# A second list for the unsplit weight loads, another bank for one tile, and a later transpose, in a two-layer hybrid decoder trunk

## The chip, the cores and the metric

The kernel runs on one core of a Trainium2 chip. The metric is the device time of one execution in microseconds (us). Before the change three runs took 644.15, 646.39 and 647.86 us, with a median of 646.39 us. A change of less than 0.5% (3.2 us) counts as no difference here.

The core has five engines that each work off their own list of instructions, in the order in which it was written: TensorE (PE, matrix products into PSUM), VectorE (DVE), ScalarE (ACT), GpSimd (POOL) and SyncE (SP), which issues nearly all transfers from HBM. They meet at semaphores.

## The reference, cut to what matters

Two layers, each of them a mixer and a feed-forward block, on x of 256 tokens by 1024 features:

```
proj = rmsnorm(x, norm_mix) @ w_in          # 1024 x 3476, its columns shared out to the head groups
qk   = silu(causal_conv([m_q, m_k], conv_qk))
y_m  = mlstm(qk, m_v, m_o, gates)           # chunked linear attention, 4 heads of 128
y_b  = moba(rope(rmsnorm(b_q)), ..)         # block attention; with 256 tokens, plain causal
y_n  = nsa(n_q, n_kc, n_vc, ..)             # three branches: compressed, selected, window
x    = x + [y_m, y_b, y_n] @ w_out
x    = x + square(relu(rmsnorm(x, norm_ffn) @ w_ff1)) @ w_ff2
```

The compressed branch of `nsa` runs blocks of 32 tokens, with `cmp_pe` added, through a small network (`cmp_w1` of 2048 x 128 for keys and for values, `cmp_w2`). These are the "compressed layer" of the change. The convolution vectors are `conv_qk`.

## The kernel before, in words

**Products in pieces.** Float32 products are made of faster ones. A weight piece arrives in a `raw` tile (4 buffers; 128 x 1024 floats at most). ACT casts it to `hi` (fp32r), DVE subtracts to get `lo`; each has 6 buffers. Each product is three matmuls, activation-high by hi, activation-high by lo, activation-low by hi (`passes`). A `raw` buffer is free again when its `lo` is made, a `hi` and `lo` pair when PE has used it. The pieces of `cmp_w1` are used as they come, without a split; they go into tiles `whole` (2 buffers), and the set of their numbers is also called `whole`.

**Groups.** A layer takes the columns of `w_in` in the order of `ORDER`: o1 (compressed inputs and NSA queries), o6 (output gates), o2 (NSA keys, values and gates), o3 (mLSTM gates and MoBA queries), c0 and c1 (compressed layer, first half), q0 (convolution inputs), c2 and c3 (second half), o4, q1, q2, q3, o5. `project` does a group named o: two tiles of 128 tokens (i = 0, 1), each of which sums over 8 slices of the features in one PSUM bank of the kind `acc` (2 of them); a tile's bank is free when its sums have been read out. `project_t` does a q group in one `acc` bank. All short-lived PSUM tiles are of the kind `wk` (6 banks). `compress` multiplies two `cmp_w1` pieces at a time.

**What sets the order.** The whole program is written by a planner, `Flow`. Every helper is a generator that yields operations, requests for buffers, and names of events to wait for. `Flow.run` keeps an estimated clock for each engine, and takes next the operation that could start first, or one of smaller rank that is ready nearly as soon. So an edit to one helper can change the order on all engines. The planner's clock sets the order only; on the chip each engine waits at its semaphores for as long as it takes.

**Loads.** One generator, `loads`, runs over all pieces in the order of their use, and requests a buffer, `raw` or `whole`, for each before it goes on to the next. The instructions of all loads stand on SP.

**Small vectors.** `first` loads `norm_mix`, then `norm_ffn` and `conv_qk` into a tile `dg` (2 buffers), has PE turn them (`wk<-ident,dg`) and copies them to `V`. `first_smalls` loads the gains of the head norms into `GB` by three broadcast DMAs (moba, nsa_q, nsa_k), scales two of them by 1/8 on DVE, and loads and turns `cmp_pe`.

Of the kernel before, what the change touches and what calls it, by code (L numbers as in the profile page):

```python
# [29 lines left out]
ORDER = ("o1", "o6", "o2", "o3", "c0", "c1", "q0", "c2", "c3", "o4", "q1", "q2", "q3", "o5")  # L30
# [114 lines left out]
class Flow:  # L145
# [16 lines left out]
    def add(self, gen, rank):  # L162
        self.procs.append([rank, gen, None, None, 0.0])
# [7 lines left out]
    def free(self, *tiles):  # L171
        for t in tiles:
            name = t.tensor.name
            self.places[self.owner.pop(name)].append(self.used.get(name, ("", 0.0))[1])
# [107 lines left out]
def body(ctx, tc, x, w_in, b_if, conv_qk, m_norm, moba_g, nsa_qg, nsa_kg, cmp_pe, cmp_w1, cmp_w2,  # L282
# [11 lines left out]
    done, free, add = flow.done, flow.free, flow.add  # L294
# [6 lines left out]
    def new(tag, *shape, dt=F32):  # L301
        return New(tag, (128, *shape), dt)

    def wk(*shape, count=1):
        return New("wk", (128, *(shape or (512,))), F32, count)
# [3 lines left out]
    def keep(tag, *shape, dt=F32, parts=128):  # L309

        if tag not in kept:
            kept[tag] = cp.tile([parts, *shape], dt, tag=tag, name=tag)
        return kept[tag]

    def tokens(i):
        return slice(i * 128, (i + 1) * 128)
# [107 lines left out]
    whole = {j for j, p in enumerate(pieces) if len(p[0]) == 2}  # L424
# [1 line left out]
    coming = [0, 0]  # L426
    taken = [0]

    def loads():
        for j, (srcs, kk, n) in enumerate(pieces):  # L430
            if j < 4:
                yield f"x0{j % 2}{j // 2}"
            raw = yield new("whole" if j in whole else "raw", 1024)
            raws[j] = raw
            for src, a in srcs:
                dst = raw[:, :kk * n] if a is None else raw[:, a * 512:(a + 1) * 512]
                yield sy.dma_start(dst.rearrange("p (k n) -> p k n", n=n), src)
            done.add(f"raw {j}")
# [36 lines left out]
    def weights():  # L475

        j = taken[0]
        taken[0] += 1
        yield f"lo {j}"
        if j >= SPLIT0:  # L480
            yield f"los {j}"
        _, kk, n = pieces[j]
        t = parts.pop(j)
        return tuple(a[:, :kk * n].rearrange("p (k n) -> p k n", k=kk) for a in t) + (t,)
# [48 lines left out]
    def passes(po, hx, lx, wh, wl, first, last):  # L533
        yield mm(po, hx, wh, start=first, stop=False)
        yield mm(po, hx, wl, start=False, stop=False)
        yield mm(po, lx, wh, start=False, stop=last)

    def project(l, name, n):

        L = Ls[l]  # L540
        po = L.o.setdefault(name, [])
        ws = []
        order = [(i, k) for i in range(2) for k in range(8)]
        if l == 0 and name == ORDER[0]:

            order = [(i, 2 * j + k) for j in range(4) for i in range(2) for k in range(2)]
        for i, k in order:
            if k == 0:
                po.append((yield new("acc", 512)))
            yield f"H{l}{i}{k}"  # L550
            if len(ws) == k // 2:
                ws.append((yield from weights()))
            elif l == 0 and name == ORDER[0] and k // 2 < SPLIT0:
                yield f"los {k // 2}"
            wh, wl, t = ws[k // 2]
            hx, lx = (a[:, k, tokens(i)] for a in (L.Hh, L.Hl))
            yield from passes(po[i][:, :n], hx, lx, wh[:, k % 2, :], wl[:, k % 2, :], k == 0, k == 7)
            done.add("started")
            if i and k % 2:
                free(*t)  # L560
            if k == 7:
                done.add(f"{name}{l}{i}")
# [148 lines left out]
    def main():  # L711
        for l in range(DEPTH):
            for name in ORDER:
                if name in ("c0", "c2"):
                    yield from compress(l, int(name[1]))
                elif name[0] == "c":
                    continue
                elif name[0] == "q":
                    yield from project_t(l, int(name[1]))
                else:  # L720
                    yield from project(l, name, GROUPS[name][1])
            yield from out_project(l)
            yield from feed_forward(l)
# [4 lines left out]
    def first():  # L728
        yield sy.dma_start(ident, cst[:, 0:128])
        v = (yield new("dg", 128))  # L730
        yield ac.dma_start(v[0:16], norm_mix.rearrange("l (k p) -> (l k) p", p=128))

        warm = keep("warm", 1)
        yield gp.memset(warm, 0.0)
        yield act(warm, warm, AF.Exp)
        for h in range(2):
            c = slice(h * 512, (h + 1) * 512)
            for i in range(2):
                yield sy.dma_start(xs[i][:, c], x[tokens(i), c])
                done.add(f"x0{i}{h}")  # L740
                yield f"raw {2 * h + i}"
        yield dv.memset(ones, 1.0)
        yield dv.memset(negh, -0.5)
        yield gp.memset(Ls[0].mr.bitcast(F32), 0.0)

        vps = yield wk()
        yield tr(vps[:, :16], v[:16], ident[:16, :16])
        yield dv.tensor_copy(V[:, :16], vps[:, :16])
        free(vps)
        done.add("V")  # L750
        yield "started"
        yield sy.dma_start(v[16:32], norm_ffn.rearrange("l (k p) -> (l k) p", p=128))
        yield sy.dma_start(v[32:96], conv_qk.rearrange("l j (c p) -> (l j c) p", p=128))
        vps = yield wk()
        yield tr(vps[:, :NV], v[:NV], ident[:NV, :NV])
        yield dv.tensor_copy(V[:, 16:], vps[:, 16:NV])
        free(vps, v)
        done.add("V2")
# [551 lines left out]

    tiles = [(i, n) for i in range(2) for n in range(2)]
    add(first(), -1)
    add(warm_up(), 101)
    for i, n in tiles:
# [4 lines left out]
    for l in range(DEPTH):  # L1319
# [4 lines left out]
        gens += [mlstm(l)] + [conv(l, c) for c in range(4)] + [attention(l, moba), score(l, moba)]  # L1324
        for g in gens:
            add(g, 2 + len(flow.procs))
    add(loads(), 95)

    def turn(j, ahead):

# [31 lines left out]
```

## Time and profile before

| | |
|---|---|
| three runs | 644.15, 646.39, 647.86 us |
| the profiled execution | 643.21 us |
| its span, first to last instruction | 641.4 us |
| PE busy (matmul) | 632.2 us, 99% |
| DVE, ACT busy | 442.8 us (69%), 368.9 us (58%) |
| granted TensorE clock, mean | 0.999 |

The profiled execution lies 1.81 us above its span and 3.18 us below the median of the three runs. In the timeline a row is a run of equal instructions: start in us from the span's start, time from the start of the first to the end of the last, engine, line, operation, output<-inputs, size, count, and in brackets the idle time of the engine just before and what ended it. Nearly all instructions have line L137, where the planner's wrapper calls the engine, so that tiles tell them apart. Matmuls are pipelined: a row's time is longer than the step from one start to the next.

### The profile page before, as it was taken

To read this page: it belongs to the slowest core of one execution; us is meant where nothing else is said; L and a number is where in the kernel's file an instruction comes from. 1 tells how busy PE (TensorE), PEld (TensorE's weight loads), DVE (VectorE), ACT (ScalarE), POOL (GpSimd) and SP (SyncE) were. 2 spreads that over 40 slices of the span, in tenths; PEclk is the share of its full clock that TensorE was granted. 3 is DMA by queue.
4 is the path that set the end of the run, shared out by engine and by line. 5 is a ranking of instruction groups with operands and counts; after the bars stand their busy time and mean duration, and the time that the engine had idled before them with its cause. 6 is when DMAs were issued, how large, how long until landed. Compare 5 with 4: busy or idle time off the path is not lost.

```text
span 641.4 us, 10239 instructions
## 1 busy us (share of the span) xinstructions
PE 632.2 (99%) x3815; PEld 544.5 (85%) x3815; DVE 442.8 (69%) x823; ACT 368.9 (58%) x718; POOL 30.9 (5%) x50
## 2 busy tenths in 40 slices
PE   9999999999999999999999999999999999999997
PEld 8788898888888888888899978988888888888885
DVE  6667898678666565656584689987776565665661
ACT  6659796547464454545384797856555553545440
POOL 1020300100000000000010111001000000000000
PEclk9999999999999999999999999999999999999999
DMA  8876724446646465655446654354566656574621
GB/s 270 221 217 205 207 92 159 137 132 228 218 154 223 158 226 169 200 195 184 144 131 183 216 167 129 103 175 127 159 230 191 203 171 215 161 225 150 223 71 66
DMA packets 79090, 112.78 MB, mean 176 GB/s; under 512 B 4896, under 2 KB 61248, under 8 KB 79040
## 3 DMA queue, kind: packets, MB, share of 16 engines
q1 hardware_dynamic: 79008, 112.12, 55.6%
q8 instruction: 30, 0.49, 0.3%
q14 instruction: 20, 0.16, 0.1%
q10 hardware_dynamic: 32, 0.01, 0.0%
HBM read 111.06 MB, written 1.05 MB: 175 GB/s over the span
## 4 chain that ended last, share of the span: by engine, by line
PE 85%; ACT 4%; DMA 3%; DVE 3%; issue 2%; POOL 1%; SPq 1%; DVEq 0%; POOLq 0%; ACTq 0%
PE wk L137 53%; PE acc L137 32%; DMA raw<-in_w_in 2%; DVE lo L137 1%; ACT hi L137 1%; ACT P L137 1%; DMA x<-in_x 1%; POOL hr L137 1%; SPq L136 1%; DMA dg<-in_cmp_pe 1%; DVE N L137 1%; ACT L137 1%; ACT QK L137 0%; ACT W L137 0%; DVE P L137 0%
## 5 line engine op out<-in xcount | busy, mean ns | idle before, releaser
L137 DVE TENSOR_TENSOR lo<-raw,hi 128x1024 fp32r<-128x1024 f32 (+4 forms) x209 | 240.5, 1167 | 124.7 <-ACT hi L137 123.9
L137 ACT CAST hi<-raw 128x1024 fp32r<-128x1024 f32 (+3 forms) x207 | 205.8, 1016 | 138.2 <-PE wk L137 110.8
L137 PE MATMUL wk<-H,hi 128*128 128x512 f32 x512 | 128.0, 391 | 0.0
L137 PEld LDWEIGHTS wk<-H,hi 128*128 128x128 f32 x512 | 93.7, 188 | 17.9
L137 PE MATMUL acc<-hi,H 128*128 128x512 f32 (+3 forms) x384 | 104.9, 353 | 0.5 <-ACT R L137 0.5
L137 PE MATMUL acc<-hi,P 128*128 128x512 f32 x240 | 79.3, 391 | 0.1
L137 PE MATMUL wk<-hi,P 128*128 128x512 f32 x240 | 78.8, 389 | 0.0
L137 PEld LDWEIGHTS wk<-H,lo 128*128 128x128 f32 x512 | 69.9, 190 | 5.0
L137 PEld LDWEIGHTS acc<-hi,H 128*128 128x128 f32 x384 | 66.9, 188 | 7.4 <-ACT R L137 0.8
L137 PE MATMUL wk<-H,lo 128*128 128x256 f32 x512 | 71.4, 282 | 0.0
L137 PE MATMUL acc<-lo,H 128*128 128x512 f32 (+3 forms) x192 | 68.3, 356 | 0.5 <-DVE lo L137 0.4
L137 PEld LDWEIGHTS acc<-hi,P 128*128 128x128 f32 x240 | 45.0, 188 | 9.4 <-DVE P L137 0.7
L137 PEld LDWEIGHTS wk<-hi,P 128*128 128x128 f32 x240 | 45.1, 188 | 9.3
L137 PE MATMUL acc<-H,hi 128*128 128x256 f32 x256 | 50.1, 288 | 1.1 <-ACT R L137 1.1
L137 PE MATMUL acc<-lo,P 128*128 128x512 f32 x120 | 47.0, 392 | 0.0
L137 PE MATMUL wk<-lo,P 128*128 128x512 f32 x120 | 46.7, 389 | 0.0
L137 ACT COPY th<-wk 128x256 f32<-128x256 f32 x64 | 23.8, 372 | 33.8 <-PE wk L137 33.8
L137 PEld LDWEIGHTS acc<-H,hi 128*128 128x128 f32 x256 | 40.1, 190 | 1.6 <-ACT R L137 1.3
L137 PEld LDWEIGHTS acc<-lo,H 128*128 128x128 f32 x192 | 36.1, 188 | 4.6 <-DVE lo L137 1.0
L137 PE MATMUL acc<-H,lo 128*128 128x256 f32 x128 | 37.5, 293 | 0.0
L137 ACT ACTIVATE H<-wk,V 128x128 fp32r<-128x128 f32 x64 | 18.5, 372 | 24.2 <-PE wk L137 24.2
L137 ACT CAST P<-cv 128x512 fp32r<-128x512 f32 x30 | 18.7, 622 | 17.5 <-DVE cv L137 17.5
(194 smaller groups left out, 790.2 us busy)
## 6 DMA issues: line engine op xcount, KB each, us to landing
raw<-in_w_ff SPq DMA_DIRECT2D x128, 512.0 KB, 4.3
raw<-in_w_in SPq DMA_DIRECT2D x40, 512.0 KB, 4.3
raw<-in_w_out SPq DMA_DIRECT2D x16, 512.0 KB, 3.5
whole<-in_cmp_w SPq DMA_DIRECT2D x16, 256.0 KB, 4.5
raw<-in_w_in SPq DMA_DIRECT2D x8, 384.0 KB, 4.2
raw<-in_w_in SPq DMA_DIRECT2D x8, 268.0 KB, 3.3
raw<-in_w_in SPq DMA_DIRECT2D x8, 264.0 KB, 3.6
x<-in_x SPq DMA_DIRECT2D x4, 256.0 KB, 5.3
```

The costliest lines, as they stand in the source:

```text
L136: return Op(self.name, lambda: f(out, *args), outs, [], 0.0)
L137: o = Op(self.name, lambda: f(out, *args, **kw), outs, ins, self.cost(op, outs, ins))
```

## The change

It has three parts.

1. `loads` takes a flag and is added twice. The first copy loads the split pieces, the second, with a smaller rank, the unsplit ones (`whole`). The second waits before each unsplit piece until the piece ahead of it in the common order has been issued. So a split piece no longer stands behind an unsplit one that lacks a buffer.
2. In layer 0 the tile i = 0 of the second group (o6) takes a `wk` bank instead of an `acc` bank.
3. The turn of `norm_ffn` and `conv_qk` in `first` waits until the event o600, the end of that same tile.

```
-    def loads():
+    def loads(unsplit):
         for j, (srcs, kk, n) in enumerate(pieces):
+            if (j in whole) != unsplit:
+                continue
             if j < 4:
                 yield f"x0{j % 2}{j // 2}"
+            elif unsplit:
+                yield f"raw {j - 1}"
             raw = yield new("whole" if j in whole else "raw", 1024)
...
             if k == 0:
-                po.append((yield new("acc", 512)))
+                po.append((yield new("wk" if l == 0 and name == ORDER[1] and i == 0 else "acc", 512)))
...
         yield sy.dma_start(v[32:96], conv_qk.rearrange("l j (c p) -> (l j c) p", p=128))
+        yield f"{ORDER[1]}00"
         vps = yield wk()
         yield tr(vps[:, :NV], v[:NV], ident[:NV, :NV])
...
-    add(loads(), 95)
+    add(loads(False), 95)
+    add(loads(True), 94)
```

The instructions are the same in number (3559 matmuls of the program's own count, before and now). The order changes at many places; four pieces of it matter below. Numbers behind a name tell buffers apart; they differ between the two programs.

**DVE, group o6 of layer 0.** The names `lo_334` to `lo_389` before, and `lo_331` to `lo_396` now, are the four pieces of o6. Before:

```order
L137 TENSOR_SCALAR dg_339<-ident_79,rs1_94 128x128
L137 TENSOR_TENSOR lo_334<-raw_219,hi_299 128x1024
L137 TENSOR_TENSOR lo_352<-raw_249,hi_333 128x1024
L137 TENSOR_TENSOR lo_380<-raw_289,hi_349 128x1024
L137 TENSOR_SCALAR GB_91<-GB_91 128x2x64
L137 TENSOR_TENSOR lo_389<-raw_316,hi_379 128x1024
```

Now:

```order
L137 TENSOR_SCALAR dg_336<-ident_79,rs1_94 128x128
L137 TENSOR_TENSOR lo_331<-raw_219,hi_297 128x1024
L137 TENSOR_TENSOR lo_350<-raw_248,hi_330 128x1024
L137 TENSOR_SCALAR GB_91<-GB_91 128x2x64
L137 TENSOR_TENSOR lo_381<-raw_288,hi_346 128x1024
L137 TENSOR_TENSOR lo_396<-raw_313,hi_380 128x1024
```

The scaling of `GB` stood behind the split of the third piece and now stands ahead of it.

**PE, the end of o6's first tile.** The tile is `acc_370` before and `wk_360` now; `dg_399` and `dg_392` hold `cmp_pe`, `dg_106` the convolution vectors. Before:

```order
L137 MATMUL acc_370<-lo_380,H_70 128x512
L137 MATMUL acc_370<-hi_349,H_70 128x512
L137 MATMUL acc_370<-hi_379,H_70 128x512
L137 MATMUL acc_370<-lo_389,H_70 128x512
L137 MATMUL wk_401<-ident_79,dg_399 128x64
L137 MATMUL acc_370<-hi_379,H_70 128x512 x2
L137 MATMUL acc_370<-lo_389,H_70 128x512
L137 MATMUL acc_370<-hi_379,H_70 128x512
```

Now:

```order
L137 MATMUL wk_360<-lo_381,H_70 128x512
L137 MATMUL wk_360<-hi_346,H_70 128x512
L137 MATMUL wk_360<-hi_380,H_70 128x512
L137 MATMUL wk_394<-ident_79,dg_392 128x64
L137 MATMUL wk_360<-lo_396,H_70 128x512
L137 MATMUL wk_360<-hi_380,H_70 128x512
L137 MATMUL wk_422<-ident_79,KV_344 128x128
L137 MATMUL wk_422<-ident_79,KV_369 128x128
L137 MATMUL wk_360<-hi_380,H_70 128x512
L137 MATMUL wk_360<-lo_396,H_70 128x512
L137 MATMUL wk_360<-hi_380,H_70 128x512
L137 MATMUL wk_435<-ident_79,dg_106 128x96
```

The turn of `cmp_pe` stood behind 20 matmuls of the tile and now stands behind 19; the turn of the convolution vectors, which stood in group o1, follows the tile.

**SP, from q0 to o4 of layer 0.** The 128x4x256 loads are q0's pieces, the 128x2x512 loads o4's, `whole` those of c2 and c3. Before:

```order
L136 DMA raw_514<-in_w_in 128x4x256
L136 DMA raw_521<-in_w_in 128x4x256
L136 DMA whole_687<-in_cmp_w1 128x4x128 x2
L136 DMA whole_704<-in_cmp_w1 128x4x128 x2
L136 DMA raw_718<-in_w_in 128x2x512
L136 DMA raw_729<-in_w_in 128x2x512
L136 DMA raw_747<-in_w_in 128x2x512
```

Now:

```order
L136 DMA raw_493<-in_w_in 128x4x256
L136 DMA raw_523<-in_w_in 128x4x256
L136 DMA raw_563<-in_w_in 128x2x512
L136 DMA raw_580<-in_w_in 128x2x512
L136 DMA raw_635<-in_w_in 128x2x512
L136 DMA whole_695<-in_cmp_w1 128x4x128 x2
L136 DMA whole_715<-in_cmp_w1 128x4x128 x2
```

Three of o4's loads have moved ahead of those of c2 and c3. In layer 1 the same rows have moved in the same way.

**ACT, from q0's casts to the read-out of o3's first tile, layer 0.** `hi_570`, `hi_605` before and `hi_571`, `hi_611` now are q0's pieces; `hi_642`, `hi_657` are o4's first two; `R_694<-acc_580` and `R_706<-acc_583` read out o3's first tile. Before:

```order
L137 CAST hi_570<-raw_514 128x1024
L137 CAST hi_605<-raw_521 128x1024
L137 COPY N_552<-N_552 128x4x48
L137 COPY KV_653<-N_552 128x256
L137 COPY N_594<-N_594 128x4x48
L137 ACTIVATE R_694<-acc_580,rs0_93 128x256
L137 COPY KV_697<-N_594 128x256
L137 COPY QK_73<-wk_689 128x4x128
L137 COPY QK_73<-wk_713 128x2x128
```

Now:

```order
L137 COPY N_552<-N_552 128x4x48
L137 CAST hi_611<-raw_523 128x1024
L137 CAST hi_642<-raw_563 128x1024
L137 COPY KV_662<-N_552 128x256
L137 COPY N_598<-N_598 128x4x48
L137 CAST hi_657<-raw_580 128x1024
L137 COPY KV_708<-N_598 128x256
L137 COPY QK_73<-wk_701 128x4x128
L137 COPY QK_73<-wk_721 128x2x128
L137 ACTIVATE GT0_101<-GT0_101 128x12
L137 ACTIVATE R_706<-acc_583,rs0_93 128x256
```

The read-out stood ahead of the copy `KV` and of the two copies to `QK`; it now stands behind them and behind the casts of two pieces of o4.

## Rows read from the trace of the kernel before

**Rows 1.** The page, part 1: busy us (share of the span) xinstructions.

```profile
PE 632.2 (99%) x3815; PEld 544.5 (85%) x3815; DVE 442.8 (69%) x823; ACT 368.9 (58%) x718; POOL 30.9 (5%) x50
```

**Rows 2.** Waits of PE: who waited for whom, us in total, times, longest us.

```profile
PE acc L137 <- ACT R L137: 1.5, 2, 1.1
...
PE wk L137 <- DVE PcT L137: 0.5, 1, 0.5
PE acc L137 <- DVE lo L137: 0.4, 1, 0.4
PE wk L137 <- DMA dg<-in_cmp_pe: 0.3, 1, 0.3
```

**Rows 3.** Timeline of PE, group o6, first tile, layer 0.

```profile
18.54 0.50 PE L137 MATMUL acc<-hi,H 128*128 128x512 f32 x1 [0.46 <-ACT R L137]
...
21.68 0.40 PE L137 MATMUL acc<-lo,H 128*128 128x512 f32 x1
...
23.05 0.39 PE L137 MATMUL acc<-lo,H 128*128 128x512 f32 x1
23.70 0.27 PE L137 MATMUL wk<-ident,dg 64*128 64x64 f32 x1 [0.26 <-DMA dg<-in_cmp_pe]
23.90 0.73 PE L137 MATMUL acc<-hi,H 128*128 128x512 f32 x2
```

**Rows 4.** Timeline of SP, the loads of nsa_q's gains and of cmp_pe.

```profile
16.50 0.43 SPq L136 DMA_DIRECT2D GB<-in_nsa_q_norm  x1
...
19.43 0.50 SPq L136 DMA_DIRECT2D dg<-in_cmp_pe  x1
```

**Rows 5.** DMA issues of 16 to 19.9 us: KB each, median us from issue to landing.

```profile
GB<-in_nsa_q_norm SPq DMA_DIRECT2D x1, 32.0 KB, 4.7
dg<-in_cmp_pe SPq DMA_DIRECT2D x1, 32.0 KB, 4.2
```

**Rows 6.** Timeline of DVE, third piece of o6 and the scaling of GB.

```profile
20.19 1.23 DVE L137 TENSOR_TENSOR lo<-raw,hi 128x1024 fp32r<-128x1024 f32 x1 [1.26 <-ACT hi L137]
21.34 0.22 DVE L137 TENSOR_SCALAR GB<-GB 128x128 f32<-128x128 f32 x1
```

**Rows 7.** Timeline of PE, the turn of the convolution vectors in o1.

```profile
12.14 0.59 PE L137 MATMUL acc<-hi,H 128*128 128x384 f32 x2
12.58 0.25 PE L137 MATMUL wk<-ident,dg 96*128 96x96 f32 x1
12.60 0.42 PE L137 MATMUL acc<-lo,H 128*128 128x384 f32 x1
12.86 0.51 PE L137 MATMUL acc<-hi,H 128*128 128x384 f32 x2
```

**Rows 8.** Timeline of ACT, from q0's casts to the copies to QK, layer 0.

```profile
40.63 1.05 ACT L137 CAST hi<-raw 128x1024 fp32r<-128x1024 f32 x1 [2.70 <-DMA raw<-in_w_in]
41.97 1.05 ACT L137 CAST hi<-raw 128x1024 fp32r<-128x1024 f32 x1 [0.28 <-DMA raw<-in_w_in]
...
43.82 0.40 ACT L137 COPY KV<-N 128x256 f32<-128x256 f32 x1 [0.56 <-DVE N L137]
...
45.27 0.47 ACT L137 ACTIVATE R<-acc,rs 128x256 f32<-128x256 f32 x1 [0.73 <-DVE GI L137]
...
45.94 1.11 ACT L137 COPY QK<-wk 128x512 f32<-128x512 f32 x2
```

**Rows 9.** Timeline of PE, start of q0, second half of the compressed layer, o4.

```profile
45.80 0.50 PE L137 MATMUL acc<-H,hi 128*128 128x256 f32 x2 [1.08 <-ACT R L137]
...
55.11 1.08 PE L137 MATMUL wk<-whole,MQ 128*32 128x128 f32 x32
...
57.90 0.50 PE L137 MATMUL acc<-lo,H 128*128 128x512 f32 x1 [0.42 <-DVE lo L137]
```

**Rows 10.** Timeline of SP, the loads of q0, then of c2 and c3.

```profile
34.18 2.32 SPq L136 DMA_DIRECT2D raw<-in_w_in  x2
43.33 2.02 SPq L136 DMA_DIRECT2D whole<-in_cmp_w  x4
```

## The prediction

> **What bounds the kernel now.** Read the busy times first: PE is busy for 632.2 of 641.4 us [rows 1]. A change that leaves the matmuls as they are can win only what PE waits, so the second view is PE's waits. The longest entries are small: 1.5 us on ACT's read-out R in two waits, 0.5 on a copy PcT, 0.4 on a lo, 0.3 on the load of cmp_pe [rows 2]. The third view is PE's timeline, which says where they lie. The two waits on R are the first matmul of o6, idle 0.46 us [rows 3], and the first of q0, idle 1.08 us [rows 9]; together they are all of the 1.5, so layer 1 has no such wait. The lo wait is o4's second matmul [rows 9], the load wait the turn of cmp_pe inside o6 [rows 3]. Last come ACT, DVE and SP around these places, since they decide what is late next.
>
> What the change aims at is thus 0.46 (the bank), 0.26 (the turn of cmp_pe) and 0.42 (o4's pieces): 1.1 us, 0.2% of the time. What it can lose is not bounded that way, because it rearranges in-order engines that feed PE.
>
> **Part 1, group o6: bank and convolution vectors.** The turn of the convolution vectors leaves o1: between 12.14 and 12.86 PE does three matmuls and that turn in 0.72 us [rows 7]. A 512-column matmul takes 0.228 (six from 21.68 to 23.05 [rows 3]), so three of 384 columns are an estimated 0.51 and the turn costs 0.2. Without it and without the idle 0.46, o6 starts 0.66 us sooner, at 17.88. The fourteenth matmul, the first that reads the third piece's lo, came 3.14 us after the start, at 21.68 [rows 3], and could now come at 21.02. But that lo ends at 20.19 + 1.23 = 21.42 [rows 6], and its cast on ACT is not moved. Even with DVE's order as it was, only 0.26 of the 0.66 is left.
>
> DVE's order is not as it was: the scaling of GB now stands ahead of that lo. It waits for the gains of nsa_q, issued at 16.50 [rows 4] and landed 4.7 us later [rows 5], at 21.2. The rows before hide this, as the scaling came at 21.34, behind the lo [rows 6]. Now DVE, which was idle for 1.26 us before that lo [rows 6], stands at the scaling until 21.2, and behind it are queued the third and fourth lo, for which PE waits. The scaling takes 0.22, overlapping the next by 0.08 as before [rows 6], so the lo runs from 21.35 to 22.6, and the fourteenth matmul comes at 22.6, not 21.68. Six steps on, at 22.6 + 6 x 0.228 = 23.97, stands the turn of cmp_pe, whose load (19.43 [rows 4] + 4.2 [rows 5] = 23.6) is in by then: its idle 0.26 is gone, in the shadow of the larger wait. Before, that turn came at 23.70 with 20 matmuls done [rows 3]; now 0.27 later with 19, which is 0.50 behind. The turn of the convolution vectors comes back for 0.2. Part 1 as a whole: 0.7 us late. Bounds: if nsa_q lands as fast as cmp_pe, 4.2, then 0.4; if it takes as much longer, 1.2. I take 0.7, by its own row.
>
> Here a rule speaks the other way. The Trainium skill, page "DMA: Bandwidth & Descriptors", section "Anatomy of one DMA — SWDGE (gpsimd) path", gives a DMA as about 2.0 us fixed plus bytes over 436 GB/s, fitted on the GpSimd path. By it nsa_q's 32 KB would land at an estimated 18.6 and cmp_pe's at 21.5, and block nothing: the fourteenth matmul would follow the lo's end at 21.45, the turn six steps later at 22.8 without a wait, and part 1 would win an estimated 0.45. Those loads took 4.7 and 4.2 us here [rows 5], among other loads of SP's queue, and I go by these.
>
> The later V copy on DVE is needed by the convolution after q0 and hidden there; if that cover went, it would cost its few tenths. The wk bank lent to o6 leaves five for short-lived tiles during 6 us in which few are open; I cost it at nothing, and a missing bank would show as a wait of the size of those seen, 0.3 to 0.5 [rows 2].
>
> **Part 2, q0: loads of o4 ahead.** Before, SP was done with q0's loads at 34.18 + 2.32 = 36.5 and stood until 43.33, for a `whole` buffer [rows 10]. Now o4's first two loads fill that gap. q0's casts both start on a landing, 40.63 and 41.97, so a 512 KB piece lands every 1.34 us [rows 8]; o4's first two would land at 43.3 and 44.65. Part 1 shifts PE by 0.7, and with it the casts that need PE's buffers and the loads behind them: 44.0 and 45.35. The shift could be 0 (if the queue, not the buffers, sets the loads) or 1.2.
>
> The planner now writes the casts of these pieces ahead of work that PE needs. ACT takes the first at 44.0 to 45.05, then KV (0.40) and a copy of that kind, then the second, until then landed, from 45.8. Behind it stand KV 0.40, two QK copies 1.11, a short GT of 0.2, and only then the read-out R of 0.47 [rows 8], whose bank q0's first matmul waits for. Neighbours on ACT overlap by 0.1 (R and KV, 0.47 and 0.40, fill 45.27 to 45.94, 0.67). So R ends at 45.8 + 1.05 + 0.40 + 1.11 + 0.2 + 0.47 - 0.5 = 48.55. PE followed R's end by 0.06 (45.74 to 45.80), so q0 starts at 48.6 instead of 45.80 [rows 9]: 2.8 us late, part 1's 0.7 included. Bounds: with the loads not shifted 2.1; with both casts waiting on nothing, their 2 us alone, 1.9; with the full 1.2 shift 3.3. The old wait of 1.08 stays inside: it grows, it does not go.
>
> c2 and c3 are now loaded behind three o4 loads. Their issue ended at 43.33 + 2.02 = 45.35 and PE used them at 55.11: 9.8 us of cover [rows 9, 10]. Three loads at 1.34 take 4.0 of it, and PE is later itself, so this costs nothing. Were the cover gone, each us beyond it would be one of PE.
>
> **Part 3, o4.** Its pieces are split long before use, so the idle 0.42 [rows 9] goes, with 0.1 for the restart: 0.5 won.
>
> **Layer 1.** Only the loads part acts there. By the order, one cast of o4, not two, stands ahead of R; PE did not wait for R there. I take 0. Bounds: 0.5 won (the PcT wait [rows 2]) and 2 lost.
>
> **Sum.** 2.8 - 0.5 = 2.3 us late. 643.2 + 2.3 = 645.5 for an execution like the profiled one; that one lies 3.2 below the median of its three runs, so 648.7, +0.35%.
>
> **The rivals.**
>
> A: the change does what it aims at. PE's three waits of 1.1 us go and nothing takes their place: 646.4 - 1.1 = 645.3. For it: the rows of the waits. Against it: the 0.26 cap of part 1, and the casts on ACT.
>
> B: part 1 as forecast, but ACT gets to R as early as before, because o4's pieces land well before their casts and DVE, which it waited for (0.73 on GI [rows 8]), had room for them; that idle time speaks for it. Then 0.7 - 0.5 = 0.2 late: 646.6. Against it: the landings 1.34 apart leave no room.
>
> C, slower: layer 1 pays as well. Place: q0 of layer 1, where the same three o4 loads have moved ahead. Price: the two casts ahead of PE's work, 1.05 each [rows 8], 2.1 us more: 650.8, +0.7%. It decides from the point where R, or DVE's work for the gates behind the o4 splits, ends after PE has come to q0. Against it: no wait on R there before, and loads that run further ahead.
>
> D: the two small loads are in early, nsa_q before 20.19, when DVE took the third lo [rows 6], and cmp_pe before its turn. Part 1 then wins instead of losing, but q0 starts where o4's landings put it, 2.1 late (part 2's bound without a shift): 2.1 - 0.5 = 1.6 late, 648.0. For it: such a small load has little to move. Against it: 4.7 and 4.2 us in the rows [rows 5]. The Trainium skill's rule for one DMA, above, is on this side.
>
> **How the numbers follow.** Forecast 0.55, A 0.12, B 0.14, C 0.14, D 0.05. The forecast's own range is 646.6 to 650.4: its bounds, and about 1 us for a median of runs that differ by 3.7. The range for 8 in 10 is 645.0 to 651.0. Faster by over 0.5% means under 643.2, which asks for more than all the aimed waits: 0.04. Slower by over 0.5% means above 649.6: a quarter of the forecast, most of C and a little of B and D, 0.27. Within 0.5%: 0.69.
>
> **What would show it.** In o6, DVE idle of about 2 us ahead of the scaling of GB, released by a DMA, and PE waiting for a lo of about 1.5 us; against it, a scaling that starts before 19.5. At q0, PE idle of 3 us before its first matmul, released by ACT's R, with two casts of o4 ended by landings before it; against it, q0 starting within 1.5 us of 45.8. At o4, no wait on a lo. The forecast is wrong if PE's waits in sum are smaller than before, or if layer 1 has a wait of over 1 us of its own.

## The result, and the profile after

The changed kernel took 650.73 us (median of 14 executions, 647.83 to 653.32), the kernel before, on the same chip, 643.98 us (14 executions). The ratio is 1.0094, with a 95% interval of 1.0078 to 1.0111: about 6.1 us slower by the ratio (the two medians lie 6.75 apart), and more than the 0.5% that counts. The forecast, 2.3 us slower and 648.7 us, had the sign, but called it most likely too small to tell.

The profiled execution took 649.26 us, with a span of 647.5 us against 641.4. Two parts of the page of the changed kernel: busy time of PE, which answers to [rows 1], and the granted clock in 40 slices of the span.

```profile
PE 634.5 (98%) x3815; PEld 546.8 (84%) x3815; DVE 443.5 (68%) x823; ACT 368.5 (57%) x718; POOL 31.2 (5%) x50
...
PEclk9997999999999999999999999999999999999999
```

PE is busy 2.3 us longer with the same matmuls. The 7 in the fourth slice says that they ran there at a lower clock; before, all 40 digits are 9. Next, PE's waits of the changed kernel (in total, times, longest), against [rows 2]:

```profile
PE acc L137 <- ACT R L137: 2.1, 1, 2.1
PE wk L137 <- DVE lo L137: 2.0, 1, 2.0
PE wk L137 <- ACT KV L137: 1.8, 1, 1.8
```

The load of cmp_pe and the lo of o4 are gone, as meant. In their place stand a lo of 2.0 in a `wk` tile (that is o6), a KV of 1.8, and one R of 2.1. Where they lie is read from the starts of PE's rows in layer 0:

| PE starts, us | before | after | later by |
|---|---|---|---|
| o6 | 18.54 | 17.66 | -0.89 |
| o2 | 30.88 | 31.85 | +0.97 |
| compressed layer, first half | 42.62 | 43.59 | +0.97 |
| q0 | 45.80 | 49.57 | +3.77 |
| compressed layer, second half | 55.11 | 61.44 | +6.33 |
| o4 | 56.54 | 62.45 | +5.91 |
| feed-forward | 146.17 | 152.32 | +6.15 |
| layer 1, q0 | 359.09 | 365.57 | +6.48 |
| last matmul | 636.49 | 642.64 | +6.15 |

There are three steps: 0.97 in o6, 2.80 in front of q0, and 2.56 between q0 and the second half of the compressed layer, where nothing waits that did not wait before. After that, all is moved as a block, within 0.4 us. (o4's 5.91 is a change of order: four transposes, 0.42 us, stood between the second half and o4's first matmul, and now stand behind it.)

**The step in o6.** DVE's timeline of the changed kernel (start, time, engine, line, operation, tiles, count, idle time before) answers to [rows 6]:

```profile
21.38 0.23 DVE L137 TENSOR_SCALAR GB<-GB 128x128 f32<-128x128 f32 x1 [2.59 <-DMA GB<-in_nsa_q_norm]
21.52 2.98 DVE L137 TENSOR_TENSOR lo<-raw,hi 128x1024 fp32r<-128x1024 f32 x3
```

SP's timeline of the same kernel, against [rows 4], with the next load of a piece:

```profile
16.36 0.43 SPq L136 DMA_DIRECT2D GB<-in_nsa_q_norm  x1
...
22.77 1.50 SPq L136 DMA_DIRECT2D raw<-in_w_in  x2
```

PE's timeline, against [rows 3], with the turn of cmp_pe in the second row:

```profile
22.79 0.50 PE L137 MATMUL wk<-lo,H 128*128 128x512 f32 x1 [2.01 <-DVE lo L137]
...
24.38 0.27 PE L137 MATMUL wk<-ident,dg 64*128 64x64 f32 x1
```

DVE stands 2.59 us at the scaling of GB until nsa_q's gains land, 4.93 us after their issue at 16.36 (at 21.29), with the third and fourth lo behind it. PE waits 2.01 us for the third. There is a second effect that the forecast left out: a `raw` buffer comes free when its lo is made, and SP's next load of a piece goes out at 22.77 instead of 21.45 (over the whole span, 393.6 us of SP's waits are for a lo). The view by windows shows what the transfers lose. Its columns are the stretch and its length, busy time and count of PE, PEld, DVE, ACT and POOL, granted clock, DMA share and GB/s. Of the kernel before:

```profile
22.00:24.00 2.00, 1.74 (x9) 1.09 (x7) 1.20 (x2) 1.08 (x2) 0.00 (x0) 1.00 0.80 214
```

And of the changed kernel:

```profile
22.00:24.00 2.00, 1.21 (x5) 1.03 (x6) 2.00 (x3) 1.04 (x2) 0.00 (x0) 1.00 0.33 63
```

214 GB/s fell to 63 in that window. Loads follow each other closely up to q0, whose first one goes out at 36.59 instead of 34.18. It landed at 42.66, not 40.61: 2.05 us late, where PE was only 0.97 late.

**The step at q0.** ACT's timeline of the changed kernel, against [rows 8]:

```profile
42.69 1.05 ACT L137 CAST hi<-raw 128x1024 fp32r<-128x1024 f32 x1 [2.95 <-DMA raw<-in_w_in]
...
44.05 1.05 ACT L137 CAST hi<-raw 128x1024 fp32r<-128x1024 f32 x1
45.43 1.04 ACT L137 CAST hi<-raw 128x1024 fp32r<-128x1024 f32 x1 [0.33 <-DMA raw<-in_w_in]
46.38 0.40 ACT L137 COPY KV<-N 128x256 f32<-128x256 f32 x1
...
46.94 1.04 ACT L137 CAST hi<-raw 128x1024 fp32r<-128x1024 f32 x1
47.88 0.40 ACT L137 COPY KV<-N 128x256 f32<-128x256 f32 x1
48.19 0.84 ACT L137 COPY QK<-wk 128x512 f32<-128x512 f32 x2
48.93 0.22 ACT L137 ACTIVATE GT<-GT 128x12 f32<-128x12 f32 x1
49.05 0.47 ACT L137 ACTIVATE R<-acc,rs 128x256 f32<-128x256 f32 x1
```

And PE's, against [rows 9]:

```profile
46.83 0.44 PE L137 MATMUL wk<-ident,KV 128*128 128x128 f32 x2 [1.79 <-ACT KV L137]
47.10 0.39 PE L137 MATMUL wk<-ident,N 128*128 128x128 f32 x2
49.57 0.80 PE L137 MATMUL acc<-H,hi 128*128 128x256 f32 x2 [2.07 <-ACT R L137]
```

The first two casts are q0's, the next two (45.43, 46.94) o4's. KV stands behind the first of these, R behind both, and behind another KV, two QK copies and GT. PE waits 1.79 us for KV and 2.07 for R, with 0.66 us of transposes between.

**The step behind q0.** The windows of the changed kernel show the cause in the third column from the end, the granted clock:

```profile
46.00:48.00 2.00, 0.66 (x4) 0.40 (x4) 2.00 (x12) 2.00 (x5) 0.00 (x0) 1.00 0.95 247
48.00:50.00 2.00, 0.43 (x2) 0.43 (x3) 2.00 (x6) 2.00 (x6) 0.00 (x0) 0.71 1.13 341
50.00:52.00 2.00, 2.00 (x11) 1.67 (x12) 2.00 (x7) 1.03 (x3) 0.00 (x0) 0.50 1.11 370
...
54.00:56.00 2.00, 2.00 (x16) 2.00 (x15) 1.24 (x3) 0.79 (x3) 0.00 (x0) 0.58 1.04 355
56.00:58.00 2.00, 2.00 (x20) 2.00 (x19) 0.30 (x3) 1.99 (x7) 0.00 (x0) 1.00 0.42 149
```

Towards the end of the two waits, before q0's first matmul, the clock falls from 1.00 to 0.50, that is from 2.4 to 1.2 GHz, and is back only from 56 us on. A 256-column matmul then takes a step of 0.21 us instead of 0.12. From q0's first matmul to the second half of the compressed layer the same work, but for two transposes that now stand ahead of q0, takes 11.87 us instead of 9.31.

Each execution comes with its mean granted clock. All 14 of the changed kernel lie between 0.990 and 0.995. Of the kernel before (27 executions beside the first experiments), 16 had 0.998 or more and 11 had 0.993 to 0.997. A small part of such a mean is the end of the program: PE's last matmul of the kernel before starts at 636.49, and the windows of its last microseconds read:

```profile
640.00:641.40 1.40, 0.00 (x0) 0.00 (x0) 0.00 (x0) 0.00 (x0) 0.00 (x0) 0.50 0.02 6
```

So a mean of 0.998 need not be a fall that cost anything. Of the 14 profiled executions of this document, the eight with 0.998 or more show no fall before PE's last matmul, and the six with 0.997 or less each show one, around q0's start. That the other executions fall at the same place is likely, but no trace shows it.

### The profile page after: what moved, and what is told of

Read it like the earlier page. It is cut to its first block, busy times and chain, and to the rows that moved or that the text cites. A ratio compares the mean times of both kernels' runs of the same rounds, so it can differ in the third digit from the quotient of the medians.

```text
span 647.5 us, 10258 instructions
## 1 busy us (share of the span) xinstructions
PE 634.5 (98%) x3815; PEld 546.8 (84%) x3815; DVE 443.5 (68%) x823; ACT 368.5 (57%) x718; POOL 31.2 (5%) x50
## 4 chain that ended last, share of the span: by engine, by line
PE 85%; DMA 5%; DVE 3%; ACT 2%; issue 2%; POOL 1%; SPq 1%; DVEq 0%; POOLq 0%; ACTq 0%
PE wk L137 52%; PE acc L137 34%; DMA raw<-in_w_in 3%; DMA GB<-in_nsa_q_norm 2%; DVE lo L137 1%; POOL hr L137 1%; ACT hi L137 1%; SPq L136 1%; DVE N L137 0%; DVE H L137 0%; ACT VC L137 0%; POOL rs L137 0%; DVE x L137 0%; ACT R L137 0%; ACT th L137 0%
## 5 line engine op out<-in xcount | busy, mean ns | idle before, releaser
L137 PE MATMUL acc<-hi,H 128*128 128x512 f32 (+3 forms) x368 | 100.4, 352 | 0.0
L137 PEld LDWEIGHTS acc<-hi,H 128*128 128x128 f32 x368 | 64.1, 188 | 6.9 <-issue 0.9
L137 PE MATMUL acc<-lo,H 128*128 128x512 f32 (+3 forms) x184 | 64.7, 352 | 0.0
L137 PEld LDWEIGHTS acc<-lo,H 128*128 128x128 f32 x184 | 34.6, 188 | 2.8 <-issue 0.2
L137 ACT CAST P<-cv 128x512 fp32r<-128x512 f32 x30 | 18.6, 621 | 17.7 <-DVE cv L137 17.7
```

What stands on the lines that cost most here:

```text
L137: o = Op(self.name, lambda: f(out, *args, **kw), outs, ins, self.cost(op, outs, ins))
```

## The experiments

The theory: the scaling of GB, put ahead of the third lo of o6, delays lo pieces and through the raw buffers the loads. The late loads and o4's casts then keep KV and R from PE, and the waits take the clock down. The rivals: that the list of loads does it by itself, or that the late part is not the clock. Ratios are to the kernel before on the same chip.

### Which of the three edits

Part 1 of the change alone (`loads`, and the last hunk, on the kernel before):

```
+            if (j in whole) != unsplit:
+                continue
...
+    add(loads(False), 95)
+    add(loads(True), 94)
```

> The kernel before with the list of loads of its own alone; the bank and the turn of the convolution vectors are as before. Theory (ACT takes two casts of o4 ahead of KV and R, and the two waits then take TensorE's clock down): the first matmul of o2 stays at 30.9 us; q0's first matmul comes about 2.8 us later than before, at 48.6, with PE idle of 1.5 to 2 us in front of KV and again in front of it; the granted clock falls to about 0.5 in the 4 to 6 us behind, so that the second half of the compressed layer comes 5.3 late; o4 without a wait on lo; in all 4.5 to 5 us longer than before, 0.7 to 0.8%. Rival (the 0.97 us that group o6 carries over is needed for the collision): q0 less than 1 us later, granted clock at 1.00 throughout, at most 0.5 us longer.

Measured: 644.96 against 645.01 us, ratio 1.0006 (0.9988 to 1.0024). The rival is right on the time and the clock, and with it goes a part of my reasons: the list by itself costs nothing that can be told. ACT's timeline around q0 in this kernel:

```profile
41.35 1.05 ACT L137 CAST hi<-raw 128x1024 fp32r<-128x1024 f32 x1 [2.67 <-DMA raw<-in_w_in]
...
44.10 1.05 ACT L137 CAST hi<-raw 128x1024 fp32r<-128x1024 f32 x1
45.05 0.40 ACT L137 COPY KV<-N 128x256 f32<-128x256 f32 x1
45.37 1.05 ACT L137 CAST hi<-raw 128x1024 fp32r<-128x1024 f32 x1
...
46.57 0.47 ACT L137 ACTIVATE R<-acc,rs 128x256 f32<-128x256 f32 x1
```

And PE's:

```profile
45.51 0.44 PE L137 MATMUL wk<-ident,KV 128*128 128x128 f32 x2 [0.68 <-ACT KV L137]
...
47.09 0.51 PE L137 MATMUL acc<-H,hi 128*128 128x256 f32 x2 [0.93 <-ACT R L137]
```

The two casts of o4 (44.10, 45.37) do stand ahead of R, but wait for no landing, and here the planner put R right behind the second. q0 starts 1.3 late in this execution, more than the rival allowed; 0.75 of it comes from before 43 us, and the execution ends 1.0 us later than the profiled one of before (span 642.4 against 641.4). The clock stays at 1.00.

The turn of the convolution vectors alone:

```
         yield sy.dma_start(v[32:96], conv_qk.rearrange("l j (c p) -> (l j c) p", p=128))
+        yield f"{ORDER[1]}00"
```

> The kernel before with the later turn of the convolution vectors alone. Theory (it is this edit, and not the bank, that puts the scaling of GB ahead of the third lo of o6): DVE stands about 2.6 us idle ahead of that scaling, PE waits about 1.5 us for lo, o6 still starts behind R near 18.5 (0.4 idle), and o2's first matmul comes 0.9 to 1.0 late, since the landing of nsa_q's gains sets it whatever the start; the second part of the first layer is shifted by the same 1 us and its clock stays at 1.00; in all 1.0 us longer, 0.15%. Rival (the bank moves the scaling): o2's first matmul within 0.2 us of 30.88, and no difference in all.

Measured: 646.25 us, ratio 1.0027 (1.0008 to 1.0047). DVE's timeline in o6:

```profile
20.97 0.23 DVE L137 TENSOR_SCALAR GB<-GB 128x128 f32<-128x128 f32 x1 [2.08 <-DMA GB<-in_nsa_q_norm]
```

So this small edit alone moves the scaling, and DVE stands 2.08 us. o2 comes 0.58 late (0.9 to 1.0 expected), and the clock of this execution stays at 1.00; four of the eight have 0.994 to 0.997.

The bank alone:

```
-                po.append((yield new("acc", 512)))
+                po.append((yield new("wk" if l == 0 and name == ORDER[1] and i == 0 else "acc", 512)))
```

> The bank alone. Theory: DVE's order in o6 stays that of before, the scaling of GB behind the third lo; o6 starts without waiting for R, 0.3 to 0.5 sooner, of which o2 keeps at most 0.3, since the third lo comes when it came; in all 0 to 0.4 us shorter than before, which cannot be told from none. Rival (the bank moves the scaling as well as the turn does): DVE idle over 2 us ahead of the scaling, and 1 us longer.

Measured: 644.29 us against 644.73, ratio 1.0005 (0.9984 to 1.0026); o6 starts 0.82 sooner (0.3 to 0.5 expected) and o2 keeps 0.21 of it. The scaling stays where it was. As the theory had it: nothing to be told.

Bank and turn, with the old loads:

```
-    def loads(unsplit):
+    def loads():
...
-    add(loads(False), 95)
-    add(loads(True), 94)
+    add(loads(), 95)
```

> The changed kernel with the loads in the one old list: the bank and the later turn alone. Theory (the stall of DVE in o6 costs about 1 us by itself, and only together with o4's loads in front of c2 and c3 does it become 5 or 6): DVE idle 2 to 2.6 us ahead of the scaling of GB, o2's first matmul 0.6 to 1 late; KV and R on ACT with no cast of o4 ahead of them, q0's first matmul 1.0 to 1.6 late; mean granted clock 0.997 to 0.999; in all 1.0 to 1.5 us longer than before. Rival (the stall alone is enough for the fall of the clock, and the loads add only their casts): mean clock 0.995 or less and 3 us or more longer than before.

Measured: 648.07 us (5 executions), ratio 1.0054 (1.0038 to 1.0070), mean clock 0.993 to 0.997. That is more than my theory gave and near what the rival asks; the stall weighs more than the 1 us that I gave it (o2 comes 1.53 late here). DVE's timeline in o6:

```profile
21.95 0.23 DVE L137 TENSOR_SCALAR GB<-GB 128x128 f32<-128x128 f32 x1 [3.07 <-DMA GB<-in_nsa_q_norm]
```

ACT's ahead of q0:

```profile
44.09 1.05 ACT L137 CAST hi<-raw 128x1024 fp32r<-128x1024 f32 x1 [3.79 <-DMA raw<-in_w_in]
...
47.27 0.41 ACT L137 COPY KV<-N 128x256 f32<-128x256 f32 x1 [0.79 <-DVE N L137]
...
48.72 0.47 ACT L137 ACTIVATE R<-acc,rs 128x256 f32<-128x256 f32 x1 [0.73 <-DVE GI L137]
```

No cast of o4 stands ahead of KV and R here. It is q0's own first piece that lands late, with ACT idle for 3.79 us: cast at 44.09, q0's first matmul at 49.25. The clock then falls to 0.50 between 50 and 52 us. Whether the bank adds to the turn (1.0027 and 1.0054) stays open: the intervals overlap, and the landing of nsa_q's gains differs from one execution to the next.

### The scaling of GB held

```
-            yield ts(GB[:, 0:3:2], GB[:, 0:3:2], 0.125, None, op0=ALU.mult)
+            if l:
+                yield ts(GB[:, 0:3:2], GB[:, 0:3:2], 0.125, None, op0=ALU.mult)
...
         free(pps, per)
+        yield "lo 7"
+        yield ts(GB[:, 0:3:2], GB[:, 0:3:2], 0.125, None, op0=ALU.mult)
         done.add("s00")
```

> The changed kernel, with the scaling of GB in layer 0 held until the fourth lo of o6 is made and cmp_pe has been copied. Theory (one stall on DVE starts it all: the lo pieces come late, so the raw buffers come free late, so the loads of q0 and o4 land 2 us late and collide with KV and R): no idle time of DVE of over 1.5 us in o6; o2's first matmul at 30.3 to 30.8 us instead of 31.85; q0's loads land near 41 instead of 42.7; two casts of o4 still stand ahead of the first R, but q0's first matmul comes by 47.1; mean granted clock 0.997 or more; in all about 5 us shorter than the changed kernel, at 645.3 or so, no different from before. Rival (the collision at q0 lies in the list of loads itself): o2 gains the same 1 us, but PE still waits 3 us or more in front of q0, the clock falls, and the time stays above 648.

Measured: 644.81 us against 644.53, ratio 1.0002 (0.9981 to 1.0023), with all three parts of the change in place. Of ten executions seven had a mean clock of 1.000, one 0.998 and two 0.995. DVE's timeline shows no stall at the scaling, which stands behind four lo pieces of o6 and two of o2 now:

```profile
20.44 2.36 DVE L137 TENSOR_TENSOR lo<-raw,hi 128x1024 fp32r<-128x1024 f32 x2 [1.27 <-ACT hi L137]
...
25.25 0.22 DVE L137 TENSOR_SCALAR GB<-GB 128x128 f32<-128x128 f32 x1
```

With the scaling held, the whole loss is gone. The edit does not part the stall from the order at q0, though: the scaling's place changes the planner's order there too, and R stands right behind the second cast of o4, as with the loads alone. The other kernels help. The five with the scaling ahead of the third lo (the changed kernel, the turn alone, bank and turn, and the two below with the casts held and with the waits filled) have ratios of 1.0027 to 1.0094, each with an interval above 1. The five with it behind and no fill (the loads alone, the bank alone, this one, and the two of "Versions that might win") have 0.9989 to 1.0006, none told from 1. So no loss is seen without the stall. With the stall and no cast of o4 ahead of KV and R, the loss is 1.7 to 3.5 us (the turn alone, casts held, bank and turn); the full 6.1 came only with the changed kernel's order at q0.

The profiled execution itself is one of the two at 0.995 (648.01 us; KV waits 1.83 there and the clock falls). So the places that I gave for o2 (30.3 to 30.8; 31.26 seen), for q0's first landing (near 41; 42.12 seen) and for q0 (47.1; 47.86 seen) were missed in it, and the verdict rests on the times of all ten. Its first load of q0 did go out at 34.41, as early as before, but took 7.7 us to land instead of 6.4.

### At q0: the casts, and the clock

o4's casts of layer 0 held until the read-out R:

```
             yield f"raw {j}"
+            if 22 <= j < 26:
+                yield "bq00"
             hi = yield new("hi", 1024, dt=F32R)
```

> The changed kernel, with the casts of o4's pieces of the first layer held until both of o3's read-outs are planned as far as the first R; the loads stay ahead. Theory (the two casts ahead of KV and R are the whole cost at q0): KV and R come on ACT right behind q0's casts, q0's first matmul falls back to 46.8 to 47.2 us, the 1 us that group o6 carries over and no more; the granted clock stays at 1.00; o4 may wait up to 0.5 us for a lo again; in all 5 us shorter than the changed kernel, 0.6 to 1.5 us longer than before. Rival (R is held by DVE and by the landings, not by the casts' place): q0's first matmul stays later than 48.5, the clock falls again, and no more than 1.5 us come back.

Measured: 646.86 us, ratio 1.0031 (1.0007 to 1.0056): some 4 us come back, not 5. q0's first matmul comes at 47.09, as expected, but the clock still fell in this execution, against the expectation (0.50 between 48 and 50 us), and over ten executions the mean clock is 0.993 to 1.000, eight of them 0.997 or less.

Over the runs without fill, the time from the cast of q0's first piece, which starts when that lands, to q0's first matmul goes by the order of the work that ACT does in between (with short waits for DVE in it, 0.73 on GI in [rows 8]):

| kernel | cast of q0's first piece | q0's first matmul | between |
|---|---|---|---|
| before | 40.63 | 45.80 | 5.17 |
| turn alone | 42.17 | 47.34 | 5.17 |
| bank and turn | 44.09 | 49.25 | 5.16 |
| casts held | 41.93 | 47.09 | 5.16 |
| loads alone | 41.35 | 47.09 | 5.74 |
| scaling held | 42.14 | 47.86 | 5.72 |
| changed | 42.69 | 49.57 | 6.88 |

The 3.77 us at q0 are thus 2.06 for the late landing, 0.57 for o4's casts ahead of R, and 1.14 for a KV, two QK copies and GT that the changed kernel puts ahead of R as well. The executions without fill that the table leaves out (the bank alone, and those of "Versions that might win") have 5.15 or 5.16 as well. The first of the three numbers is of one execution each. In the profiled executions without a stall of over 2 us at the scaling, this cast starts between 40.09 and 42.71; with one, between 42.17 and 44.09. The size of that part is therefore uncertain by about 1 us. SP's issues tell the link more cleanly than the landings: the next load of a piece behind cmp_pe's goes out between 21.09 and 21.94 in the nine profiled executions with the scaling behind the third lo, and between 22.36 and 23.34 in the five with it ahead; q0's first load goes out between 34.13 and 35.46, and between 35.26 and 36.72. From there to its landing it takes 5.7 to 7.9 us, and that differs from one execution to the next.

PE kept busy in the two waits, with the order unchanged:

```
+    def busy(o, call, ahead, behind):
+        def go():
+            for _ in range(ahead):
+                tc.nc.tensor.matmul(o, B[:, :128], B[:, :128], start=True, stop=True)
+            r = call()
+            for _ in range(behind):
+                tc.nc.tensor.matmul(o, B[:, :128], B[:, :128], start=True, stop=True)
+            return r
+        return go
...
-                yield tr(pt[:, b, :], a.rearrange("p a d -> p (a d)"), ident)
+                t = tr(pt[:, b, :], a.rearrange("p a d -> p (a d)"), ident)
+                if L is Ls[0] and i == 0 and len(pairs) == 6 and (b0, b) in ((0, 2), (4, 1)):
+                    t.call = busy(pt[:, 2, :], t.call, 30 if b0 == 0 else 0, 35 if b0 else 0)
+                yield t
```

> The changed kernel with 30 bf16 matmuls of 128 columns in front of the transposes of KV and 35 in front of q0's first matmul, in the same order otherwise; their results are not read, and no part of the computation is left out. Theory (what the two waits cost behind them is the granted clock, because PE stood still): the casts of o4 still come first, and KV and R end when they did, so q0's first matmul stays at 49.5 us (within 0.4); the granted clock is 1.00 between 48 and 56 us, the 256-column steps take 0.12 and not 0.21, and the stretch from q0's first matmul to the second half of the compressed layer takes 9.3 us as before and not 11.9; in all 2.5 us shorter than the changed kernel, about 648.2. Rival (the slower steps come from something else that moved there, the transfers or the order of the work): the stretch stays at 11.9 us and the time that of the changed kernel.

Measured: 648.21 us, ratio 1.0057 (1.0037 to 1.0077), so 2.4 us of the 6.1 are gone. The mean clock of its eight executions is 0.996 to 1.000, five of them at 0.998 or more, where none of the changed kernel's 14 had more than 0.995. The windows behind q0's start:

```profile
50.00:52.00 2.00, 1.50 (x13) 1.33 (x15) 2.00 (x7) 1.94 (x5) 0.00 (x0) 1.00 1.10 315
52.00:54.00 2.00, 2.00 (x31) 1.88 (x30) 1.48 (x2) 1.97 (x5) 0.00 (x0) 1.00 1.04 366
54.00:56.00 2.00, 2.00 (x20) 2.00 (x19) 0.92 (x4) 1.97 (x6) 0.00 (x0) 1.00 1.06 360
```

PE's timeline, with the fill on the lines of `busy`:

```profile
45.02 1.84 PE L879 MATMUL wk<-B 128*128 128x128 bf16 x30
...
47.45 2.12 PE L882 MATMUL wk<-B 128*128 128x128 bf16 x35
50.51 0.50 PE L137 MATMUL acc<-H,hi 128*128 128x256 f32 x2 [0.94 <-ACT R L137]
```

The clock stays at 1.00 in all windows, and the stretch from q0 to the compressed layer takes 9.10 us, in the same order in which it took 11.87. PE did no useful work more than before, and q0 even came 0.94 later than in the changed kernel, against the expectation: the QK copy of ACT waited for the fill (idle 0.72). So the third step is the clock, and with PE kept busy in the two waits it does not come.

### Versions that might win

The whole change with the scaling held and the casts held (both edits above):

```
+            if 22 <= j < 26:
+                yield "bq00"
...
+        yield "lo 7"
+        yield ts(GB[:, 0:3:2], GB[:, 0:3:2], 0.125, None, op0=ALU.mult)
```

> The whole change, with the scaling of GB held behind the lo pieces of o6 and o4's casts of layer 0 held until the first read-out of o3 is planned. Theory: neither stall nor collision, q0's first matmul 0 to 1 us from before's 45.8, mean clock 0.998 or more, time within 0.6 us of before. Rival (with the casts held PE waits for lo at o4, and with the scaling late for cmp_pe's sums): 1 us or more longer.

Measured: 645.04 us against 644.73, ratio 1.0002 (0.9983 to 1.0022). The time is as expected, but the mean clock of its 12 executions averages 0.998, between 0.995 and 1.000, and in the profiled one, at 0.995, q0 comes 2.06 late where 0 to 1 was expected: the repairs do not free it of falls.

Bank and loads, without the turn, with the casts held:

```
-        yield f"{ORDER[1]}00"
...
+            if 22 <= j < 26:
+                yield "bq00"
```

> The bank and the list of loads, without the later turn of the convolution vectors, and with o4's casts of layer 0 held until the first read-out of o3 is planned. Theory: nothing is left of the two collisions; o6 starts 0.4 earlier, o2's first matmul comes 0.2 to 0.4 earlier than before, q0's first within 0.5 of before's 45.8, o4 without a wait on lo of over 0.2; mean granted clock 0.998 like before; in all 0.4 to 0.8 us shorter than before, which is near what can be told. Rival (held casts make o4 late and leave PE waiting for other things, as in the run with casts held before, whose mean clock was 0.996): 0.5 to 1.5 us longer than before.

> The bank and the list of loads without the later turn, casts of o4 held, once more with more rounds: the run before gave a ratio of 0.9989 with an interval of 0.9964 to 1.0014. Theory (it is faster than before by the waits at o6 and o4, 0.9 us): ratio 0.9980 to 0.9992, with 1 outside the interval. Rival (the waits removed come back as others, as the profile of that run has KV at 1.1 us): ratio 0.9995 to 1.0010.

Measured: 0.9989 (0.9964 to 1.0014), and in the second run 1.0003 (0.9987 to 1.0020). So the rival of the second holds. The aimed waits come back as others: in the first, PE waits 1.1 us for KV, and q0's first matmul comes at 47.18, where it was expected within 0.5 of 45.8. No version tried is faster than the kernel before.

That version and the kernel before, with 12 and 18, or 8 and 18, matmuls of fill. This fill writes into the bank that holds the compressed layer's sums and spoils them, so that these two kernels are read for times and clocks alone; the other work stays.

```
-            L.z = yield wk(128)
+            L.zt = yield wk()
+            L.z = L.zt[:, :128]
...
+                    t.call = busy(L.zt[:, 256:384], t.call, 12 if b0 == 0 else 0, 18 if b0 else 0)
```

> The same as the run before it (bank, list of loads, held casts), and 12 bf16 matmuls of 128 columns in front of the transposes of KV and 18 in front of q0's first matmul, into unused columns of the bank that holds the compressed layer's sums; their results are not read. Theory (where executions of one kernel differ, it is by falls of the granted clock behind the waits in front of q0; executions of before had mean clocks of 0.993 to 1.000, mean 0.998, and the times went with them): the mean clock is 0.999 or more in all executions, and the time is 1.0 to 1.8 us below before, 643.5. Rival (the clock falls at other places too): mean clock 0.998 and the time of the run without the fill.

> The kernel before with 8 and 18 such matmuls at the same two places and nothing else. Theory: the waits of PE in front of q0 stay, 1.1 us and a little, and q0's first matmul comes at 45.8 to 46.0; but the granted clock no longer falls behind them in any execution: mean clock 0.999 or more, mean time 1 to 1.3 us below before, and a spread of 2 us instead of 4.5. Rival (what falls there are in executions of before lie elsewhere): mean clock 0.998, same time and spread as before.

Measured: 645.22 and 645.05 us against 644.53, ratios 1.0002 (0.9983 to 1.0021) and 1.0000 (0.9982 to 1.0018). Both expectations failed on the time. PE's timeline of the kernel before with this fill shows a reason:

```profile
46.45 0.51 PE L137 MATMUL acc<-H,hi 128*128 128x256 f32 x2 [0.66 <-ACT R L137]
...
47.13 1.17 PE L876 MATMUL wk<-B 128*128 128x128 bf16 x18
```

The 18 matmuls do not stand where they were meant to. In these two kernels the transposes that they hang on come behind q0's first matmuls, so the wait for R in front of q0 stays empty (0.66 us, and 0.38 in the other kernel), and the fill lies in the middle of q0. From q0's first matmul to the second half of the compressed layer it takes 10.39 us in both, against 9.31 in the kernel before, with the clock at 1.00. So the fill itself cost about 1.1 us, and the times do not test the idea. The clocks speak for it, weakly: one of the ten executions of the kernel before with fill has 0.997 or less, against 13 of the 31 without; of the other version two of ten, as without the fill in its first run (six of twelve in its second). Where the clock falls in those executions of the kernel before that have 0.993 to 0.997 was not seen in a trace, and stays open.

## Why the prediction was right or wrong

- **Part 1, group o6: right in mechanism, order and place.** A DVE stall of about 2 us at GB released by a DMA was forecast, 2.59 came; a PE wait for lo of 1.5, 2.01 came; 0.7 late in all, 0.97 came, inside the bounds of 0.4 to 1.2. cmp_pe's load no longer waits. The prediction gave part 1 as a whole; the runs show that the turn moves the scaling and the bank does not.
- **Part 2, q0: the right waits, mis-sized.** The forecast was 2.8 late, 3.77 came. The step that failed is "Part 1 shifts PE by 0.7, and with it the casts that need PE's buffers and the loads behind them: 44.0 and 45.35". The pieces of o4 landed at 45.35 and 46.62. The loads do not move with PE: they wait for raw buffers, which DVE's lo frees, and DVE stood still. The bounds for the shift, 0 to 1.2, did not reach the 2.05 seen, though landings of single executions differ by 1 us or more without the stall too. The list of casts and copies ahead of R was right item by item. (The sum for R's end, put at 48.55, adds up to 48.53; nothing hangs on it.)
- **The missing term.** The sum has no line for the granted clock. It charged the wait and took the matmuls behind it at their old steps. 2.56 us came there in the profiled execution, and filling the waits gave back 2.4 in the times. That is the larger half of the 3.8 us by which the sum (2.3) missed the measured 6.1; the rest is q0's 0.97 and o4's 0.3.
- **Part 3, o4: the wait went, less was won.** o4 has no wait on a lo, as forecast. Of the 0.5 that this was to win, 0.2 is left by the feed-forward (6.15 late, against 6.33 at the compressed layer): PE waits 0.17 us for an N at 82 us, where it did not wait before.
- **Layer 1: right.** 0 was forecast; its q0 and its out-projection stand within 0.4 us of the block's shift. So rival C is out, and that its 650.8 is nearly the time that came is chance. A and B fall with q0's wait. D falls with the landing of nsa_q after 4.93 us. The rule of the Trainium skill that D drew on (page "DMA: Bandwidth & Descriptors", section "Anatomy of one DMA — SWDGE (gpsimd) path") put that landing at an estimated 18.6; the trace does not agree, here (21.29) as before (21.2).
- **The chances.** 0.69 for no difference was too sure. All bounds were bounds of waits, added up as if what follows a wait were unaffected. That 650.73 still lies in the range of 645.0 to 651.0 is luck: its base, 646.39, was the median of three runs, and moved to the 643.98 of 14 executions the sum gives 646.3 and the range ends at 648.6.

## What to carry to other kernels

Look at the landing that an in-order engine waits for ahead of its other work: here the place of one 0.2 us scaling on DVE, which waits for a small broadcast load, decided whether there was a loss, of 1.7 us or, with ACT's changed order at q0, of 6, since lo pieces, raw buffers and all loads stood behind it. When a change adds waits to PE, price the matmuls behind them at the lower clock as well, as a cost that may come, and check it by filling the wait with matmuls that nobody reads; see in the timeline that the fill stands in the wait, and write it into a bank that holds no open sums.

## What the runs showed of the hardware that was not expected

The fall of the clock is not told by the amount of waiting. The windows of the kernel with the bank alone:

```profile
44.00:46.00 2.00, 0.44 (x2) 0.20 (x2) 2.00 (x14) 1.08 (x4) 0.00 (x0) 1.00 0.79 234
46.00:48.00 2.00, 1.12 (x9) 1.12 (x10) 2.00 (x11) 1.50 (x4) 0.00 (x0) 1.00 0.89 238
48.00:50.00 2.00, 2.00 (x27) 1.71 (x26) 0.41 (x4) 1.90 (x6) 0.00 (x0) 1.00 0.99 322
```

And of the second run of the version without the turn:

```profile
44.00:46.00 2.00, 0.82 (x6) 0.34 (x4) 2.00 (x14) 0.86 (x3) 0.00 (x0) 1.00 0.66 164
46.00:48.00 2.00, 1.62 (x12) 1.62 (x13) 1.90 (x8) 1.96 (x7) 0.00 (x0) 0.92 1.08 347
48.00:50.00 2.00, 2.00 (x16) 1.67 (x16) 0.84 (x1) 1.98 (x5) 0.00 (x0) 0.50 1.16 359
```

In the first PE is busy for 1.56 of 4 us and keeps 1.00; in the second it is busy for 2.44 and falls to 0.50 right after. Executions of one kernel differ as well: of the 27 executions of the kernel before, the 16 with a mean clock of 0.998 or more took 644.2 us on average, the 11 with 0.997 or less 646.1. What decides between them is not shown by any run here.
